# Small matrix products of the delta-rule heads issued by turns of four column steps, in one block per turn

## The chip, the cores and the metric

One core of a Trainium2 chip runs the whole program in a single launch. The metric is the device time of one execution in microseconds. The engines are named as in the profile: PE multiplies matrices (PEld loads its stationary operand), DVE is VectorE, ACT is ScalarE, POOL is GpSimd, SP issues most of the DMAs. Every engine works through its own queue in order, and waits where an operand or a buffer isn't ready.

## The reference

One block of a streaming encoder, in float32, for 512 frames of width 1024. What bears on the change is the first mixer, a gated delta rule with 8 heads of width 128 (condensed):

```python
h = rmsnorm(x, norm1_w)
q, k, v, z, b, a, glu, gates = split(h @ w_in)
q, k, v = silu(causal_conv4(concat(q, k, v)))            # 4 taps, per channel
q, k = l2norm(q), l2norm(k)
# per head: S_t = a_t S_{t-1} (I - b_t k_t k_t^T) + b_t k_t v_t^T,  o_t = q_t S_t
#   by chunks: triangular systems T u = b v inside a chunk, S carried from chunk to chunk
out_a = (rmsnorm(o) * silu(z)) @ w_o
c = ga * sigmoid(gb); c = silu(layernorm(causal_conv31(c)))
out_b = c @ w_pw2 + b_pw2
x = x + (sigmoid(gate_a) * out_a + sigmoid(gate_b) * out_b) @ w_out
x = rmsnorm(x + swiglu(rmsnorm(x)), norm_f_w)
```

## The kernel before

**Large products.** Every product with a weight matrix is split: each float32 operand becomes a high and a low part, and three products (high-high, high-low, low-high) are summed in PSUM. `split3` (L114 to L121) issues the three matmuls; for one column of weights (128 output channels, all 512 frames) there are eight such threes, one for each 128 of the input width. A *column step* is one of these threes. `unit` (L101) loads a column's weights, and splits them on ACT (L111, the high part) and DVE (L112, the low part); three such buffers rotate. The PSUM tiles `mm` of the columns rotate over three buffers too.

**The queue of columns.** The first stage of the program walks a queue of generators one column step at a time (`step`, and the counter `count`). For each head it holds the columns k, q, v and z (`head`; 32 steps), and then 12 or 8 steps of other columns (`take(OTHERS[h])`: the GLU columns of the convolution branch, then the gates). After the last head the other columns are run to the end. In all there are 481 counts. When a column ends its result is taken from PSUM: for k, q and v by `conv4` (L421 on ACT, three times L424 on DVE, a Silu at L427 on ACT), for z by a Silu (L793), for a GLU column at L657 and L662, for a gate by a sigmoid. The 31-tap convolution (`conv31`, L673, 30 DVE instructions a channel block) is traced far behind and fills DVE.

**Small products.** Between these large products stand the small ones of the heads, in plain float32, 128 columns wide or less. A product of four chunks is four calls, each of them two matmuls in the profile. For a head there are

- an *opening*, `front` (L437 transposes k, L470 is k k^T; ACT takes the squares, scales and stores U; a DRAM round trip on SP spreads U; POOL solves 16x16 systems at L506 and L508 into `y`), and `front2` (L437 transposes v, L519 is k q^T, L437 transposes q), which use the two PSUM buffers `g`;
- *merges* in `chain`, from 16x16 to 128x128 inverses: L545, L551, L568, L575, L587, L592, each with copies on ACT and DVE between, in the single PSUM buffer `b` (its results are collected in `Y`);
- the *recurrence* in `chain` over the four chunks n: L605 and L606 (from the second chunk on; DVE makes R at L608), L611 (ACT scales it to w at L613), L616 and L617 (DVE makes the next state S at L621 or L623 and the output o at L626 or L630, ACT an intermediate at L629), in the single PSUM buffer `st`;
- the end, `scaled` (four ACT instructions, L645) and `finish` (L437 transposes o into `b`, DVE L651 multiplies by z).

**What sets the order.** The text gives each instruction a place, and a planner puts each engine's queue together from that place and from when it takes operands to be ready; a small product that isn't ready is passed by large ones. `behind()` adds edges: what is traced inside it is issued, on its engine, after the last marked instruction (the large matmuls on PE; the splits L111 and L112; L424, the Silus and the sigmoids). `tc.issue_after(i)` adds one such edge of issue order, without a wait for `i` to finish. Generators yield the number of column steps until they are to be called again: a recurrence step yields 3, the merges between 1 and 4, and chain `h` starts at count `START + 32 h` and the other columns so far (START is 88). `front` runs at once when q is traced and two steps of v are done, `front2` five counts after z, with its three products together. `close()` is called between columns and runs `scaled` and `finish` some 32 counts after a chain's end.

Of the kernel before, what the change touches and what calls it, by code (L numbers as in the profile page):

```python
# [6 lines left out]
F32 = mybir.dt.float32  # L7
# [7 lines left out]
P = 128  # L15
# [8 lines left out]
PAD3 = 368  # L24
START = 88
ROUND = 40
WARM = 9
# [5 lines left out]
def block_kernel(ctx, tc, a):  # L33
# [65 lines left out]
    last = [None]  # L99

    def unit(ap, pool=None):  # L101

        aps = ap if isinstance(ap, tuple) else (ap,)
        n = T * len(aps) if isinstance(ap, tuple) else 1024
        raw, hi, lo = ((pool or wp).tile([P, n if pool else 1024], t, name=x)[:, 0:n]
                       for t, x in ((F32, "raw"), (F32R, "whi"), (F32R, "wlo")))
        for i, p in enumerate(aps):
            loads.append(nc.sync.dma_start(raw[:, i * T:(i + 1) * T] if len(aps) > 1 else raw, p))
        if start_feed[0]:
            fill()  # L110
        marked(S.activation(hi, raw, AF.Copy), "unit")  # L111
        marked(V.tensor_tensor(out=lo, in0=raw, in1=hi.bitcast(F32), op=ALU.subtract), "unit")  # L112
        return hi, lo

    def split3(ps, wt, xh, xl, first, last, mv=False):

        wh, wl = wt
        terms = ((wh, xh), (wh, xl), (wl, xh))
        for i, (w, m) in enumerate(terms):
            l, r = (m, w) if mv else (w, m)  # L120
            marked(PE.matmul(ps, l, r, start=first and i == 0, stop=last and i == 2))  # L121

# [269 lines left out]
    for t in (X, Y, Q1, Q2, Xd, Yd, Yl, Ye):  # L392
        G.memset(t, 0.0)
# [40 lines left out]
    def tok(src, pool, tag):  # L434
        ps = pool.tile([P, 4, P], F32, name=tag)
        for n in range(NT):
            PE.transpose(ps[:, n, :], src[:, n, :], ident)  # L437
        return ps
# [12 lines left out]
    def front(h, kT, DT):  # L451
# [17 lines left out]
        for n in range(NT):  # L469
            PE.matmul(ps[:, n, :], kT[:, n, :], kT[:, n, :], start=True, stop=True)  # L470
        Un = gp.tile([P, NT, P], F32, name="Un", bufs=3)
# [38 lines left out]

    def front2(kT, qT, vT, DT, ss):
        nk, sq = ss[:, 5], junk[:, 0:P]
        ps = tok(vT, psg, "g")
        Vp = gp.tile([P, NT, P], F32, name="Vp", bufs=3)
        for n in range(NT):
            S.activation(Vp[:, n, :], ps[:, n, :], AF.Copy, scale=nk[:, n:n + 1])
        ps = psg.tile([P, 4, P], F32, name="g")
        for n in range(NT):
            PE.matmul(ps[:, n, :], kT[:, n, :], qT[:, n, :], start=True, stop=True)  # L519
# [5 lines left out]
        return Vp, at  # L525

    def chain(h, kT, qT, ss, kd, b2, Un, Ud, Vp, at, yq, zs):
        sq = junk[:, 0:P]

# [12 lines left out]
        yield 2  # L542
        ps = psb.tile([P, 4, P], F32, name="b")
        for n in range(NT):
            PE.matmul(ps[:, n, 0:16], Ud[:, n, :], xc[:, n, 0:16], start=True, stop=True)  # L545
        Q0 = gp.tile([P, NT, 16], F32, name="Q0")
        S.activation(Q0, ps[:, :, 0:16], AF.Copy)
        yield 2
        ps = psb.tile([P, 4, P], F32, name="b")
        for n in range(NT):  # L550
            PE.matmul(ps[:, n, 0:16], Ye[:, n, :], Q0[:, n, :], start=True, stop=True)  # L551
        V.tensor_tensor(out=xc[:, :, 0:16], in0=xc[:, :, 0:16], in1=ps[:, :, 0:16], op=ALU.add)
        V.transpose(out=flat(y), in_=flat(xc))
        yield 1
        for i in range(2):
# [3 lines left out]
        for b in range(4):  # L559
            b32 = slice(32 * b, 32 * b + 32)  # L560
            S.copy(out=Y[b32, :, b32], in_=y[b32])
            if b < 2:
                S.copy(out=X[b32, :, b32], in_=xc[b32])


        ps = psb.tile([P, 4, P], F32, name="b")
        for n in range(NT):
            PE.matmul(ps[0:64, n, 0:64], Uc[:, n, :], Xd[:, n, :], start=True, stop=True)  # L568
        for i in range(2):
            s32 = slice(32 * i, 32 * i + 32)  # L570
            S.activation(Q1[s32, :, s32], ps[s32, :, s32], AF.Copy)
        yield 3
        ps = psb.tile([P, 4, P], F32, name="b")
        for n in range(NT):
            PE.matmul(ps[0:64, n, 0:32], Q1[:, n, :], Yd[:, n, :], start=True, stop=True)  # L575
        yield 1
        for i in range(2):
# [4 lines left out]
        S.copy(out=Yl[0:64], in_=Y[64:128, :, 64:128])  # L582
        yield 4

        ps = psb.tile([P, 4, P], F32, name="b")
        for n in range(NT):
            PE.matmul(ps[0:64, n, 0:64], Un[:, n, 64:128], X[:, n, :], start=True, stop=True)  # L587
        S.activation(Q2[0:64], ps[0:64, :, 0:64], AF.Copy)
        yield 3
        ps = psb.tile([P, 4, P], F32, name="b")  # L590
        for n in range(NT):
            PE.matmul(ps[0:64, n, 0:64], Q2[:, n, :], Yl[:, n, :], start=True, stop=True)  # L592
        V.tensor_copy(out=Y[0:64, :, 64:128], in_=ps[0:64, :, 0:64])
        yield 2

# [3 lines left out]
        for n in range(NT):  # L599
# [4 lines left out]
            else:  # L604
                PE.matmul(ps[:, 0, :], kT[:, n, :], Sp, start=True, stop=True)  # L605
                PE.matmul(ps[:, 2, :], qT[:, n, :], Sp, start=True, stop=True)  # L606
# [3 lines left out]
                yield 3  # L610
            PE.matmul(ps[:, 1, :], Y[:, n, :], R, start=True, stop=True)  # L611
            w = gp.tile([P, P], F32, name="w", bufs=2)
            S.activation(w, ps[:, 1, :], AF.Copy, scale=b2[:, n:n + 1])  # L613
            yield 3
            if n < NT - 1:
                PE.matmul(ps[:, 0, :], kd[:, n, :], w, start=True, stop=True)  # L616
            PE.matmul(ps[:, 3, :], at[:, n, :], w, start=True, stop=True)  # L617
            if n < NT - 1:
# [13 lines left out]
            if n < NT - 1:  # L632
                Sp = Sn
                yield 3

# [3 lines left out]
        tc.keep_in_program_order(G.tensor_tensor(out=ss[:, 4], in0=ss[:, 3], in1=half4, op=ALU.pow))  # L639
        ended.append([count[0], False, (h, o, ss, zs)])  # L640

# [89 lines left out]

    def close():

        if ended and count[0] - ended[0][0] > ROUND - 8:
            if ended[0][1]:
                finish(*ended.pop(0)[2])
            else:
                scaled(*ended[0][2])
                ended[0][1] = True

    def gates(a, b):
        for i in range(a, b):
            close()
            yield from gate(i)
# [29 lines left out]
    def head(h, done):  # L774

        pk, pq = (yield from proj2()) if h == 0 else (None, None)
        k_ = yield from conv4(8 + h, "kT", pk)
        close()
        q_ = yield from conv4(h, "qT", pq)
        close()  # L780
        v = conv4(16 + h, "vT")
# [14 lines left out]
        def second():  # L796
            Vp, at = front2(k_, q_, v_, DT, ss)
            done.append((h, k_, q_, ss, kd, b2, Un, Ud, Vp, at, y, z_))
            yield 0

        chains.append([count[0] + 5, second()])
        yield
# [12 lines left out]

    done, ended, dts, convs, count, chains = [], [], [], [], [0], [[0, decays()]]
    rest = others()
    for h in range(H):
        queue.append(head(h, done))
        queue.append(take(OTHERS[h]))  # L820
    queue.append(rest)
    nh = 0
    while step() or chains:
        start_feed[0] = count[0] >= 335
        if nh < H and count[0] >= START + 32 * nh + sum(OTHERS[:nh]):
            chains.append([0, chain(*done[nh])])
            nh += 1
        for c in list(chains):
            if c[0] <= count[0] or not queue:
                with behind():  # L830
                    n = next(c[1], None)
                if n is None:
                    chains.remove(c)
                else:
                    c[0] = count[0] + n
    background()
    for _, sc, e in ended:
        if not sc:
            scaled(*e)
        finish(*e)  # L840
    ph1.close()

# [527 lines left out]
```

## Time and profile before

| | us |
|---|---|
| median of 3 runs | 951.96 |
| lowest and highest | 951.70, 953.46 |
| the profiled execution's own time | 951.63 |
| its span, first to last instruction | 949.9 |
| PE busy in the span | 937.8 |
| stretch from the first opening to the last finish (53 to 464 us of the span) | 411.0 |

All times inside the profile are counted from the span's start. A row of grouped instructions gives line, engine, operation, output and inputs by the program's names, shape and count, then busy time, mean nanoseconds of one, and idle time before them with what ended it. A row of the timeline gives the start, the time until the group's end, and in brackets the idle time before it. A row of the chain gives start, duration and what ran. A row of stretches gives its borders, its length, each engine's busy time with its count of instructions, the granted clock and the DMA load. PE's ends are modelled, so a pitch (from one start to the next) says more than a duration.

### The profile page before, as it was taken

The numbers are of one execution on the slowest core, as the hardware profiler recorded it, in microseconds if no ns is written. First come the engines' busy times: TensorE is split into PE (matmuls) and PEld (weight loads), VectorE is DVE, ScalarE is ACT, GpSimd is POOL, SyncE is SP. The second block draws the span as 40 slices with busy tenths as digits, with TensorE's granted clock in tenths as the row PEclk, the third lists the DMA queues.
The fourth block names the chain that finished last, engine by engine and source line by source line (L and its number), as shares of the span: only waits on it lengthen the run. The fifth ranks groups of instructions, "written<-read, shape, count | busy, mean of one in ns | idle before, by whom it ended". The sixth has DMA issues, their size and how long they took to land.

```text
span 949.9 us, 14775 instructions
## 1 busy us (share of the span) xinstructions
PE 937.8 (99%) x5144; PEld 792.7 (83%) x5144; DVE 734.9 (77%) x1141; ACT 538.2 (57%) x1117; POOL 346.3 (36%) x548
## 2 busy tenths in 40 slices
PE   9999999999999999999999999999999999999996
PEld 6778888878888888888878888988889999988885
DVE  5899898888878898899688643675636877888896
ACT  7697785867877764643547222333334554556545
POOL 1136524344353347544154350254441111143042
PEclk9999999999999999999999999999999999999999
DMA  9234322322231346979899983599898565578654
GB/s 330 101 126 121 102 88 81 102 89 91 75 94 55 126 135 155 321 215 273 267 302 293 278 255 123 181 295 290 271 249 226 181 187 183 178 227 259 212 184 149
DMA packets 78187, 177.39 MB, mean 187 GB/s; under 512 B 10080, under 2 KB 19472, under 8 KB 77088
## 3 DMA queue, kind: packets, MB, share of 16 engines
q1 hardware_dynamic: 66528, 144.89, 46.0%
q0 software_dynamic: 10288, 28.90, 13.4%
q10 hardware_dynamic: 1296, 2.67, 0.7%
q8 instruction: 40, 0.66, 0.3%
q14 instruction: 35, 0.29, 0.1%
HBM read 156.22 MB, written 45.37 MB: 212 GB/s over the span
## 4 chain that ended last, share of the span: by engine, by line
PE 86%; ACT 3%; DVE 3%; issue 2%; POOL 1%; DMA 0%; POOLq 0%; DVEq 0%; ACTq 0%; SPq 0%
PE mm L121 56%; PE w L121 20%; PE g L437 1%; DVE wlo L112 1%; PE st L611 1%; PE st L617 1%; PE b L551 1%; PE b L545 1%; PE g L470 1%; PE st L616 1%; PE st L605 1%; PE st L606 1%; PE b L587 1%; PE b L592 1%; PE b L575 1%
## 5 line engine op out<-in xcount | busy, mean ns | idle before, releaser
L111 ACT ACTIVATE whi<-raw 128x1024 fp32r<-128x1024 f32 (+1 forms) x191 | 196.6, 1030 | 249.8 <-PE mm L121 160.3
L112 DVE TENSOR_TENSOR wlo<-raw,whi 128x1024 fp32r<-128x1024 f32 (+1 forms) x191 | 241.3, 1264 | 91.8 <-ACT whi L111 90.8
L121 PE MATMUL mm<-hh,whi 128*128 128x512 f32 (+1 forms) x688 | 269.8, 393 | 0.6 <-ACT hh L336 0.3
L121 PE MATMUL mm<-hh,wlo 128*128 128x512 f32 (+1 forms) x688 | 263.3, 383 | 0.0
L121 PE MATMUL mm<-hl,whi 128*128 128x512 f32 (+1 forms) x688 | 263.1, 382 | 0.0
L673 DVE SCALAR_TENSOR_TENSOR cps<-c,c31w,cps 128x512 f32<-128x512 f32 x240 | 180.2, 751 | 6.6 <-ACT cps L671 2.3
L121 PEld LDWEIGHTS mm<-hh,wlo 128*128 128x128 f32 x688 | 129.6, 188 | 23.6
L121 PEld LDWEIGHTS mm<-hh,whi 128*128 128x128 f32 x688 | 129.7, 189 | 22.7 <-issue 0.8
L121 PEld LDWEIGHTS mm<-hl,whi 128*128 128x128 f32 x688 | 129.9, 189 | 20.7
L1003 POOL TENSOR_TENSOR fm<-fm 128x256 f32<-128x256 f32 x33 | 29.9, 907 | 115.5 <-DVE s L1003 93.6
L424 DVE SCALAR_TENSOR_TENSOR acc<-mm,c4w,acc 128x511 f32<-128x511 f32 (+2 forms) x72 | 52.9, 739 | 2.8 <-ACT acc L421 2.6
L506 POOL TENSOR_TENSOR ytm<-U,y 128x60 f32<-128x60 f32 (+14 forms) x120 | 36.4, 303 | 50.6 <-DMA U<-sc 41.9
L121 PE MATMUL mm<-yh,whi 128*128 128x512 f32 x128 | 50.6, 396 | 0.0
L121 PE MATMUL mm<-yh,wlo 128*128 128x512 f32 x128 | 49.8, 389 | 0.0
L121 PE MATMUL mm<-yl,whi 128*128 128x512 f32 x128 | 49.8, 389 | 0.0
L121 PE MATMUL w<-hh,wlo 128*128 128x256 f32 x168 | 47.7, 284 | 0.3 <-DVE wlo L112 0.3
L121 PE MATMUL w<-hh,whi 128*128 128x256 f32 x168 | 47.6, 284 | 0.0
L121 PE MATMUL w<-hl,whi 128*128 128x256 f32 x168 | 47.5, 283 | 0.0
L196 POOL DMA_DIRECT2D s<-in_wgu_dram x24 | 23.4, 990 | 63.2 <-DMA s<-in_wgu_dram 63.2
L121 PE MATMUL w<-wlo,fh 128*128 128x512 f32 (+1 forms) x115 | 44.3, 385 | 0.1
L121 PE MATMUL w<-whi,fl 128*128 128x512 f32 (+1 forms) x115 | 44.2, 385 | 0.0
L121 PE MATMUL w<-whi,fh 128*128 128x512 f32 (+1 forms) x115 | 44.2, 385 | 0.0
(333 smaller groups left out, 1915.2 us busy)
## 6 DMA issues: line engine op xcount, KB each, us to landing
raw<-in_win_dram SPq DMA_DIRECT2D x61, 512.0 KB, 3.5
raw<-in_wgu_dram SPq DMA_DIRECT2D x32, 512.0 KB, 3.8
s<-in_wgu_dram SPq DMA_DIRECT2D x48, 256.0 KB, 5.6
raw<-s SPq DMA_DIRECT2D x48, 256.0 KB, 3.6
raw<-wsum SPq DMA_DIRECT2D x44, 256.0 KB, 3.6
raw<-in_wdn_dram SPq DMA_DIRECT2D x33, 256.0 KB, 3.2
s<-in_wgu_dram POOLq DMA_DIRECT2D x24, 256.0 KB, 7.4
s<-s POOLq DMA_DIRECT2D x24, 256.0 KB, 6.9
```

The lines of the kernel that those rows point to most:

```text
L111: marked(S.activation(hi, raw, AF.Copy), "unit")
L112: marked(V.tensor_tensor(out=lo, in0=raw, in1=hi.bitcast(F32), op=ALU.subtract), "unit")
L121: marked(PE.matmul(ps, l, r, start=first and i == 0, stop=last and i == 2))
L196: fed.append(nc.gpsimd.dma_start(*begun.pop(0), accum_op=ALU.add, max_dma_last_dim=2048))
L424: marked(V.scalar_tensor_tensor(out=acc[:, s:], in0=ps[:, :T - s], scalar=c4w[:, j, k:k + 1], in1=acc[:, s:], op0=ALU.mult, op1=ALU.add))
L437: PE.transpose(ps[:, n, :], src[:, n, :], ident)
L470: PE.matmul(ps[:, n, :], kT[:, n, :], kT[:, n, :], start=True, stop=True)
L506: G.tensor_tensor(out=tm[:, :, 0:w], in0=U[:, k, :, k + 1:], in1=y[:, :, k:k + 1].broadcast_to([P, NT, w]), op=ALU.mult)
L545: PE.matmul(ps[:, n, 0:16], Ud[:, n, :], xc[:, n, 0:16], start=True, stop=True)
L551: PE.matmul(ps[:, n, 0:16], Ye[:, n, :], Q0[:, n, :], start=True, stop=True)
L673: V.scalar_tensor_tensor(out=acc, in0=c[:, k:k + T], scalar=c31w[:, i, k:k + 1], in1=acc, op0=ALU.mult, op1=ALU.add)
L1003: return eng.tensor_tensor(out=out, in0=in0, in1=in1, op=op)
```

## The change

- *Turns.* Every fourth column step is a turn: 11 fixed offsets a head, also in a head with only 8 other steps (there the last three turns are three steps apart). Small products are issued only at turns, by `take_turn`: each running chain makes one step (recurrence or merge; the number that a generator yields no longer matters), then one waiting piece of an opening, then `scaled` or `finish` of an ended chain.
- *Chains.* A chain has 18 steps, and starts 11 turns after the one before it, the first at count 75 (`FIRST - 4`). So the last seven steps of a recurrence stand in the same turns as the seven merging steps of the next head. `Y` exists twice for that. `Yd` becomes a part of `Yl`. L551's copies now stand before the turn's end, L568 in the next turn; L575 and its copies are in one step.
- *Openings.* `front` waits for the next turn; `front2` is cut into two pieces (v's transposes and L519; q's transposes), one turn apart.
- *Ends.* `scaled` follows eight turns after the chain's end, `finish` at a later turn in which no chain is merging.
- *The hold.* `small_` remembers the last small product, and the first large product traced after it gets an edge of issue order behind it.

The core of the diff:

```diff
-START = 88
-ROUND = 40
+FIRST = 79
...
+    hold = [None]
+
+    def small_(b):
+        hold[0] = b
+        return b
...
-            marked(PE.matmul(ps, l, r, start=first and i == 0, stop=last and i == 2))
+            with tc.issue_after(hold[0].ins) if hold[0] else nullcontext():
+                marked(PE.matmul(ps, l, r, start=first and i == 0, stop=last and i == 2))
+            hold[0] = None
...
-    Y = gp.tile([P, NT, P], F32, name="Y")
+    Ys = [gp.tile([P, NT, P], F32, name="Y%d" % i) for i in range(2)]
...
-    Yd = gp.tile([P, NT, 32], F32, name="Yd")
     Yl = gp.tile([P, NT, 64], F32, name="Yl")
+    Yd = Yl[:, :, 0:32]
...
-            PE.transpose(ps[:, n, :], src[:, n, :], ident)
+            small_(PE.transpose(ps[:, n, :], src[:, n, :], ident))
...
         at = gp.tile([P, NT, P], F32, name="at", bufs=3)
         V.tensor_tensor(out=at, in0=ps, in1=DT, op=ALU.mult)
+        out += [Vp, at]
+        yield 1
         ps = tok(qT, psg, "g")
...
-                yield 3
+                yield 1
...
-        with behind(), tc.issue_after(last[0].ins) if h else nullcontext():
-            ss, kd, b2, Un, Ud, y = front(h, k_, DT)
+        made = []
+
+        def opening():
+            with tc.issue_after(last[0].ins) if h else nullcontext():
+                made.append(front(h, k_, DT))
+            yield
+
+        pending.append(opening())
...
-        chains.append([count[0] + 5, second()])
+        pending.append(second())
...
+        n = 32 + OTHERS[h]
+        turns += [at_ + o for o in ((3, 7, 11, 15, 19, 23, 27, 31, 35, 39, 43) if n == 44 else
+                                    (3, 7, 11, 15, 19, 23, 27, 31, 34, 37, 40))]
+        at_ += n
+    turns += range(at_ + 3, at_ + 300, 4)
...
+    def take_turn():
+        merging = False
+        turn[0] += 1
+        for c in list(chains):
+            merging |= c[0] < 7
+            with behind():
+                if next(c[1], None) is None:
+                    chains.remove(c)
+            c[0] += 1
+        if pending:
+            with behind():
+                if next(pending[0], None) is None:
+                    pending.pop(0)
+        if ended and turn[0] - ended[0][0] > 7:
+            if not ended[0][1]:
+                scaled(*ended[0][2])
+                ended[0][1] = True
+            elif not merging:
+                finish(*ended.pop(0)[2])
...
+        if count[0] in turns or not queue:
+            if nh < H and (turn[0] - first if first is not None else 0 if count[0] >= FIRST - 4 else -1) >= 11 * nh:
+                first = turn[0] if first is None else first
+                chains.append([0, chain(*done[nh])])
+                nh += 1
+            take_turn()
```

More of the change, by code (lines that the diff above doesn't have):

```diff
@@ L796, in second @@
         def second():
[L797 to L801 removed]
+            ss, kd, b2, Un, Ud, y = made[0]
+            both = []
+            yield from front2(k_, q_, v_, DT, ss, both)
+            done.append((h, k_, q_, ss, kd, b2, Un, Ud, *both, y, z_))
+            yield
+        pending.append(second())
         yield
@@ L813, in take @@
             yield
-    done, ended, dts, convs, count, chains = [], [], [], [], [0], [[0, decays()]]
+    done, ended, dts, convs, count, pending, turn = [], [], [], [], [0], [], [0]
     rest = others()
+    turns, at_ = [], 0
     for h in range(H):
@@ L820, in block_kernel @@
         queue.append(take(OTHERS[h]))
-    queue.append(rest)
-    nh = 0
-    while step() or chains:
-        start_feed[0] = count[0] >= 335
[L825 to L835, printed above, removed]
+        n = 32 + OTHERS[h]
[3 more added lines that the diff above has]
+    turns += range(at_ + 3, at_ + 300, 4)
+    turns = set(turns)
+    queue.append(rest)
+    chains, nh, opened, dec = [], 0, [0], decays()
+    def take_turn():
[17 more added lines that the diff above has]
+                finish(*ended.pop(0)[2])
+    first = None
+    while step() or chains or pending:
+        start_feed[0] = count[0] >= 335
+        if dec and count[0] in (1, 3):
+            with behind():
+                dec = None if next(dec, None) is None else dec
+        if count[0] in turns or not queue:
[4 more added lines that the diff above has]
+            take_turn()
     background()
@@ L840, in block_kernel @@
         finish(*e)
+    hold[0] = None
     ph1.close()
```

64 lines of the change are left out of this document (26 added, 38 removed).

## The prediction

> **What bounds the kernel now.** I read the page first, then the stretch in which heads are computed, then PE's own order in it.
>
> ```profile
> span 949.9 us, 14775 instructions
> ...
> PE 937.8 (99%) x5144; PEld 792.7 (83%) x5144; DVE 734.9 (77%) x1141; ACT 538.2 (57%) x1117; POOL 346.3 (36%) x548
> ```
>
> ```profile
> 53.00:464.00 411.00, 408.67 (x2250) 335.74 (x2249) 353.55 (x636) 278.51 (x737) 189.21 (x383) 1.00 0.45 137
> ```
>
> PE is the bound: 99% of the span. The second row is the stretch that the change touches: 411.0 us long, PE busy 408.7 (its engines in order: PE, PEld, DVE, ACT, POOL), the granted clock 1.00. A busy PE can still start its matmuls late, so pitches decide. The chain of waits gives the undisturbed pitch of large products:
>
> ```profile
> 436.57 27.25 PE mm L121 x120
> ```
>
> 27.25 us / 120 = 0.227 us. The lines of the stretch hold 446 products in each of three terms:
>
> ```profile
> L121 PE MATMUL mm<-hh,wlo 128*128 128x512 f32 x446 | 176.7, 397 | 0.0
> ```
>
> 3 x 446 x 0.227 = 303.7 us, so 411.0 - 303.7 = 107.3 us go to the small products and to waiting. What one interruption costs is read from the timeline, PE alone, around two of them:
>
> ```profile
> 410.49 0.40 PE L121 MATMUL mm<-hh,wlo 128*128 128x512 f32 x1
> 410.73 0.38 PE L611 MATMUL st<-Vp,Y 128*128 128x128 f32 x2
> 410.87 0.48 PE L121 MATMUL mm<-hh,whi 128*128 128x512 f32 x1
> 411.18 0.39 PE L121 MATMUL mm<-hl,whi 128*128 128x512 f32 x1
> ...
> 412.80 0.39 PE L121 MATMUL mm<-hh,wlo 128*128 128x512 f32 x1
> 413.02 0.38 PE L616 MATMUL st<-w,kd 128*128 128x128 f32 x2
> 413.24 0.39 PE L617 MATMUL st<-w,at 128*128 128x128 f32 x2
> 413.38 0.48 PE L121 MATMUL mm<-hh,whi 128*128 128x512 f32 x1
> 413.70 0.40 PE L121 MATMUL mm<-hl,whi 128*128 128x512 f32 x1
> ```
>
> From the large product before to the second large product after, less two pitches: 411.18 - 410.49 - 0.454 = 0.236 us for two small matmuls, 413.70 - 412.80 - 0.454 = 0.446 for four. So a small matmul costs 0.105 us and **an interruption by itself only 0.026**.
>
> **The change, part by part.** *Fewer interruptions.* Walking PE's timeline I count 145 stretches of small matmuls between large ones, from the first row below to the last:
>
> ```profile
> 53.69 0.49 PE L437 MATMUL g<-cst,kT 128*128 128x128 f32 x3
> ...
> 463.66 0.60 PE L437 MATMUL b<-cst,o 128*128 128x128 f32 x4
> ```
>
> After: four turns with openings alone (heads 0 and 1), 94 consecutive turns of which each has a step of a recurrence or a merge (chain 0's second step to chain 7's last: 7 x 11 + 17), and the last head's finish: 99. The number of small matmuls does not change. 46 fewer x 0.026 = **-1.2 us**.
>
> One rule of the Trainium skill would make even this nothing: by "TensorE: Matmul & The Clock Gate", Part 2, the engine pulls weight loads ahead of matmuls in flight, so a switch of shapes should be free; then the term is 0 instead of -1.2. The two differences above say 0.026, not 0.
>
> *Waits that go.* Priced the same way, 24 of the 145 stretches cost over 0.04 us more than their own matmuls, 5.0 us together. The two kinds:
>
> ```profile
> 69.06 0.39 PE L121 MATMUL mm<-hh,wlo 128*128 128x512 f32 x1
> 69.87 0.66 PE L437 MATMUL g<-cst,qT 128*128 128x128 f32 x4 [0.43 <-ACT Vp L516]
> 70.28 0.48 PE L121 MATMUL mm<-hh,whi 128*128 128x512 f32 x1
> 70.60 0.40 PE L121 MATMUL mm<-hl,whi 128*128 128x512 f32 x1
> ...
> 272.43 0.39 PE L121 MATMUL mm<-hl,whi 128*128 128x512 f32 x1
> 273.19 0.49 PE L605 MATMUL st<-S,kT 128*128 128x128 f32 x2 [0.37 <-DVE o L630]
> 273.51 0.39 PE L606 MATMUL st<-S,qT 128*128 128x128 f32 x2
> 273.65 0.47 PE L121 MATMUL mm<-hh,wlo 128*128 128x512 f32 x1
> 273.97 0.39 PE L121 MATMUL mm<-hh,whi 128*128 128x512 f32 x1
> ```
>
> Both stretches hold four matmuls (0.446) and took 70.60 - 69.06 - 0.454 = 1.086 and the same at 273: 0.64 too much each. In the first, q's transposes wait for a PSUM buffer that v's evictions hold; six such add up to 1.8 us. After, they stand one turn later, 12 large products x 0.227 = 2.7 us. In the second, the recurrence, one step in three (9 products, 2.0 us), waits for its single PSUM tile; with the merges of a column step or two it makes 1.9 us. A turn gives 2.7 us plus the turn's own small products. I let both kinds go: **-3.7 us**; bounds 0 and all 5.0. Of the remaining 1.3 I move nothing.
>
> *The hold.* Now a small product finds its place by readiness, and large ones pass it:
>
> ```profile
> 276.43 0.80 PE b L545 x8
> 277.23 6.91 PE mm L121 x30
> ...
> 285.69 0.80 PE b L551 x8
> ```
> ```profile
> 284.17 0.21 ACT L547 ACTIVATE Q<-b 128x64 f32<-128x64 f32 x1
> ```
>
> L551 was due 6 products (1.4 us) after L545; its operand Q was copied only at 284.17, and 30 products ran in one piece meanwhile. After, the first product of the next column step stands behind the turn's last small one, and with it the rest of its column, which accumulates in order. What can still pass is another column, if its weights are split and PSUM is free. It does so today:
>
> ```profile
> 43.09 0.97 PE L121 MATMUL mm<-hh,whi 128*128 128x512 f32 x3 [0.34 <-ACT hh L336]
> ```
>
> Three first terms in a row are three columns. So in the steady state I put the hold at 0, covered by the following columns.
>
> At head 0 that cover is missing. Its opening moves to the turn after v's sixth column step, 66 products into the projections instead of 54; but k is not there yet:
>
> ```profile
> 50.97 1.28 ACT L427 ACT_TABLE_LOAD   x1
> 52.27 0.63 ACT L427 ACTIVATE kT<-acc 128x512 f32<-128x512 f32 x1
> ```
> ```profile
> 51.59 1.21 DVE L112 TENSOR_TENSOR wlo<-raw,whi 128x1024 fp32r<-128x1024 f32 x1
> ```
>
> k ends at 52.90. Counting large products on the timeline from the first one of these projections, 82 had run when the opening came at 53.69: 28 more than the 54 behind which the text has it slid past. Held behind 66, PE comes to it 16 products earlier; k lets it start about two products before 53.69, so PE lacks work for 14. The next column, z, has its low half only from 51.59 + 1.21 = 52.80; two terms of z fit before that. (14 - 2) x 0.227 = **+2.7 us**; bounds 0 (z's split comes earlier) and 3.2 (no cover).
>
> *At nothing.* The second Y replaces Yd: one more zeroing on POOL, off PE's path. Chain 0 starts 13 column steps earlier; y(0) was done long before:
>
> ```profile
> 87.29 0.21 POOL L508 TENSOR_TENSOR y<-y,ytm 128x4 f32<-128x4 f32 x1
> ```
> ```profile
> 95.97 0.34 ACT L533 ACTIVATE yb<-y,cst 128x64 f32<-128x64 f32 x1
> ```
>
> 8.5 us of slack; 13 steps are 39 products, 8.9 us, so the slack is used up and y(0) comes just in time. If it comes late, the first merge slips by what is missing, an estimated 0.4 us (8.9 - 8.5), once. No DMA is added: U's loads move with the openings by up to four column steps (2.7 us) and SP's queue order is the same; DVE and ACT execute the same instructions.
>
> Sum against the profiled execution, 951.63 us (span 949.9 and 1.7 around it): -1.2 - 3.7 + 2.7 = -2.2, so 949.4; its time is 0.3 under the median 951.96, which gives **949.7 us**.
>
> **The rivals.** *A, the holds cost (slower).* Place: the turn behind L611 of the second chunk, which comes 6 products after v's projection ends. Its eviction w is queued on ScalarE behind v's Silu:
>
> ```profile
> 254.07 0.68 ACT L421 ACTIVATE acc<-mm,c4w 128x512 f32<-128x512 f32 x1
> ...
> 262.26 0.66 ACT L427 ACTIVATE vT<-acc 128x512 f32<-128x512 f32 x1
> ...
> 263.07 0.39 ACT L613 ACTIVATE w<-st,ss 128x128 f32<-128x128 f32 x1
> ```
>
> From the start of L421 to w's end 9.4 us; L616 is due 18 products and two small ones after v's end, 4.3 us, so it is 5 us late. Over heads 2 to 7 the Silu ends 4.5 to 8.8 us after L421 starts; with w the lateness sums to 15.3 us. Six products of the next column are unheld (1.36 us a head); if nothing else passes, 8.3 us stay: 949.7 + 8.3 = 958.0. For it: eviction latencies decide, not PE. Against: three columns interleave at 43.09. It decides from the point at which the columns behind the next one have no PSUM.
>
> *B, cleaner than I think.* Head 0's hold is covered and all 5.0 us of waits go: 951.96 - 1.2 - 5.0 = 945.8. Against: this wait at head 0 is ScalarE's lateness, which no turn mends.
>
> ```profile
> PE g L437 <- ACT vT L427: 0.6, 1, 0.6
> ```
>
> *C, it does not do what it says.* Small products stay where readiness puts them, other columns fill in between, the stretches stay near 145 and waits only change places; head 0's hold against half of the 5.0 us of waits: 951.96 + 2.7 - 2.5 = 952.2.
>
> *D, the clock.* A hold that idles PE long enough costs a slow restart. At the kernel's start:
>
> ```profile
> 1.00 3.49 PE L258 MATMUL g<-one 128*128 128x512 bf16 x9 [1.00 <-DVE epsc L73]
> ```
>
> Nine took 3.49 us instead of 9 x 0.227 = 2.04: 1.45 us for a cold start; with head 0's 2.7 us and no waits saved, 951.96 + 2.7 + 1.45 - 1.2 = 954.9. The rule ("TensorE: Matmul & The Clock Gate", Part 1) halves the clock after an idle window of about 3.4 us; no wait shown here is near that, and the 2.7 would be under it.
>
> **How the numbers follow.** Forecast 0.38, A 0.20, B 0.16, C 0.23, D 0.03. A measurement here tells about 0.2% (1.9 us) from no change: 950.1 and 953.9 are the bounds. Faster: B, 0.28 of the forecast's (its own range 947 to 951.5 crosses 950.1), 0.03 of C: 0.47. Slower: A without 0.02, D, 0.05 of C: 0.26. Same: the rest, 0.27. The range leaves out half of A and the edge of B: 945.5 to 957.
>
> **What would show it.** On PE's timeline: some 99 stretches, not 145; at head 0 a gap before L437 that ends with kT (right) or none (B); no wait of L437 for Vp and none of L605 for o (the -3.7). A shows as PE idle before L616 with w as releaser, near the end of v's projections. The forecast is wrong if PE's waits in 53 to 464 grow instead of shrinking, or if the time after 464 moves.

## The result: 1.1% slower

The changed kernel takes 962.75 us (median of 4 runs, 962.0 to 963.76), the one before 952.71 us beside it (951.7 to 953.59): ratio 1.0108, 95% interval 1.0096 to 1.012. Forecast were 949.7 us and a range up to 957. The profiled execution took 962.98 us.

The same two rows of the page as before, and the same stretch by windows (us, then PE, PEld, DVE, ACT, POOL busy, PE's granted clock):

```profile
span 961.2 us, 14776 instructions
...
PE 939.5 (98%) x5144; PEld 797.3 (83%) x5144; DVE 734.0 (76%) x1141; ACT 532.6 (55%) x1113; POOL 335.5 (35%) x548
```
```profile
53.00:464.00 411.00, 399.96 (x2207) 332.67 (x2206) 351.69 (x635) 269.25 (x726) 181.40 (x382) 1.00 0.41 130
```

PE executes the same 5144 instructions. In the 411 us between 53 and 464 it was busy 408.67 us before and is busy 399.96 now: 8.7 us more in which it does nothing, and 43 matmuls fewer done (2207 against 2250), at the same full clock. All other engines did a little less too: nobody is busier, somebody waits for somebody. PE's waits by line and releaser:

```profile
PE mm L127 <- DVE acc L431: 5.4, 4, 2.2
PE g L444 <- ACT vT L434: 1.3, 2, 0.7
PE mm L127 <- DVE ss L472: 1.2, 1, 1.2
...
PE mm L127 <- DVE ss L470: 0.8, 1, 0.8
PE mm L127 <- DVE sm L761: 0.6, 1, 0.6
PE st L618 <- DVE R L615: 0.6, 1, 0.6
PE st L623 <- ACT w L620: 0.5, 1, 0.5
PE b L583 <- ACT Q L579: 0.4, 1, 0.4
```

The large waits are not those of small products. They are first products of *new columns* (L127 writing mm) that wait for a PSUM buffer until VectorE's tap instructions (L431) have read a column out. The rows that name ss or sm belong to them: in each, the instruction named stands right behind a column's last tap in VectorE's queue. Together that is 8.0 us. The old kinds, L437 for Vp and L605 for o, are gone from these rows, as forecast, though a wait for o of 0.3 us now stands at L618. The same in the page's list of groups, first the kernel before, then the changed one:

```profile
L121 PE MATMUL mm<-hh,whi 128*128 128x512 f32 (+1 forms) x688 | 269.8, 393 | 0.6 <-ACT hh L336 0.3
...
L127 PE MATMUL mm<-hh,whi 128*128 128x512 f32 (+1 forms) x688 | 271.4, 395 | 8.3 <-DVE acc L431 5.4
```

One of these places, PE, VectorE and ScalarE by the timeline:

```profile
262.85 0.38 PE L618 MATMUL st<-R,Y 128*128 128x128 f32 x2
...
265.60 0.39 PE L127 MATMUL mm<-hh,wlo 128*128 128x512 f32 x1
268.16 0.47 PE L127 MATMUL mm<-hh,whi 128*128 128x512 f32 x1 [2.17 <-DVE acc L431]
...
269.15 0.39 PE L623 MATMUL st<-w,kd 128*128 128x128 f32 x2
```
```profile
265.18 0.72 DVE L431 SCALAR_TENSOR_TENSOR acc<-mm,c4w,acc 128x511 f32<-128x511 f32 x1
...
265.96 0.74 DVE L431 SCALAR_TENSOR_TENSOR acc<-mm,c4w,acc 128x510 f32<-128x510 f32 x1
...
267.28 0.74 DVE L431 SCALAR_TENSOR_TENSOR acc<-mm,c4w,acc 128x509 f32<-128x509 f32 x1
```
```profile
266.00 1.14 ACT L480 ACTIVATE Un<-g,ss 128x128 f32<-128x128 f32 x4 [1.21 <-DVE ss L472]
268.11 0.63 ACT L434 ACTIVATE vT<-acc 128x512 f32<-128x512 f32 x1 [0.97 <-DVE acc L431]
268.65 0.35 ACT L620 ACTIVATE w<-st,ss 128x128 f32<-128x128 f32 x1
```

This is the turn behind L618 of the second chunk, rival A's place. L618's result is in PSUM at 263.2, but w, its scaled copy, is made at 268.65, right behind v's Silu (268.11) in ScalarE's queue, and that Silu waits for the last tap of v on VectorE. L623 needs w. The rows don't name the column of a product; from the order of PE's queue I read what ran meanwhile: 12 products of one column (262.99 to 265.83), until its next product is one that is held behind L623; a second column stands in the same way, with 3 products done. The third PSUM buffer still holds v, which the last tap reads until 268.02. A new column starts at 268.16, does three products, and only then comes L623. So passing did take place, 12 products of it, and ended when three buffers were all taken.

For the whole stretch I walked PE's timeline from the first product with hh to the first with yh (1440 large products of 0.227 us, 326.9 us, in each kernel) and divided what is more than that: extra time around small products (their own time and their waits), and waits between two large ones. All in us; the kernels in the lower rows follow below:

| kernel | stretches of small products | extra around small ones | waits between large ones | whole stretch |
|---|---|---|---|---|
| before | 146 | 106.4 | 3.3 | 436.5 |
| changed | 111 | 107.9 | 12.0 | 446.8 |
| changed, no hold (e1_no_hold) | 110 | 103.4 | 2.7 | 432.9 |
| changed, v's Silu free (e2_silu_free) | 110 | 104.5 | 4.1 | 435.5 |
| both (e5_both) | 111 | 102.7 | 2.8 | 432.4 |
| no hold, one-piece opening (e11_one_piece) | 113 | 104.1 | 2.6 | 433.5 |
| before, opening in two pieces (e7_before_split) | 141 | 106.8 | 3.2 | 436.9 |
| changed, a turn later (e9_hold_shift) | 109 | 113.0 | 8.9 | 448.8 |
| that, q's and v's Silus free (e13_shift_qv_free) | 105 | 106.7 | 18.4 | 452.1 |
| that, v's taps free too (e15_shift_taps_free) | 113 | 108.1 | 5.5 | 440.5 |

From before to changed: +1.5 around small products, +8.7 in waits between large ones. After the stretch nothing moved: from its end to the span's end it is 949.9 - 469.6 = 480.3 us before and 961.2 - 480.9 = 480.3 us now. Another 1.0 us lies ahead of the stretch's first product. That start falls between 33.0 and 34.9 us in the kernels of the table, with the hold or without, so I don't count it as an effect of the change.

### The profile page after: what moved, and what is told of

Its sections match the earlier page's. It is cut to its first block, busy times and chain, and to the rows that moved or that the text cites. A ratio compares the mean times of both kernels' runs of the same rounds, so it can differ in the third digit from the quotient of the medians.

```text
span 961.2 us, 14776 instructions
## 1 busy us (share of the span) xinstructions
PE 939.5 (98%) x5144; PEld 797.3 (83%) x5144; DVE 734.0 (76%) x1141; ACT 532.6 (55%) x1113; POOL 335.5 (35%) x548
## 4 chain that ended last, share of the span: by engine, by line
PE 83%; DVE 6%; ACT 3%; issue 2%; DMA 0%; POOL 0%; POOLq 0%; ACTq 0%; DVEq 0%; SPq 0%
PE mm L127 54%; PE w L127 20%; DVE acc L431 2%; DVE cps L680 2%; DVE wlo L117 1%; PE g L444 1%; PE g L526 1%; PE st L624 1%; PE b L559 1%; PE b L553 1%; ACT whi L116 1%; PE st L618 1%; PE st L612 1%; PE st L623 1%; PE g L477 1%
## 5 line engine op out<-in xcount | busy, mean ns | idle before, releaser
L127 PE MATMUL mm<-hh,whi 128*128 128x512 f32 (+1 forms) x688 | 271.4, 395 | 8.3 <-DVE acc L431 5.4
L127 PE MATMUL mm<-hh,wlo 128*128 128x512 f32 (+1 forms) x688 | 261.3, 380 | 0.0
L127 PE MATMUL mm<-hl,whi 128*128 128x512 f32 (+1 forms) x688 | 260.8, 379 | 0.0
L127 PEld LDWEIGHTS mm<-hh,whi 128*128 128x128 f32 x688 | 129.6, 188 | 33.6 <-issue 6.4
L127 PEld LDWEIGHTS mm<-hh,wlo 128*128 128x128 f32 x688 | 129.4, 188 | 25.3
L127 PEld LDWEIGHTS mm<-hl,whi 128*128 128x128 f32 x688 | 129.9, 189 | 20.6
L431 DVE SCALAR_TENSOR_TENSOR acc<-mm,c4w,acc 128x511 f32<-128x511 f32 (+2 forms) x72 | 53.2, 742 | 6.6 <-ACT acc L428 6.4
L127 PE MATMUL mm<-yh,whi 128*128 128x512 f32 x128 | 50.6, 396 | 0.0
L513 POOL TENSOR_TENSOR ytm<-U,y 128x60 f32<-128x60 f32 (+14 forms) x120 | 31.9, 266 | 52.9 <-DMA U<-sc 44.1
L127 PE MATMUL mm<-yh,wlo 128*128 128x512 f32 x128 | 49.8, 389 | 0.0
L127 PE MATMUL mm<-yl,whi 128*128 128x512 f32 x128 | 49.8, 389 | 0.0
L127 PE MATMUL w<-hh,wlo 128*128 128x256 f32 x168 | 47.7, 284 | 0.3 <-DVE wlo L117 0.3
L127 PE MATMUL w<-hh,whi 128*128 128x256 f32 x168 | 47.6, 284 | 0.0
L127 PE MATMUL w<-hl,whi 128*128 128x256 f32 x168 | 47.5, 283 | 0.0
L127 PE MATMUL w<-wlo,fh 128*128 128x512 f32 (+1 forms) x115 | 44.3, 386 | 0.1
L127 PE MATMUL w<-whi,fh 128*128 128x512 f32 (+1 forms) x115 | 44.2, 385 | 0.0
L127 PE MATMUL w<-whi,fl 128*128 128x512 f32 (+1 forms) x115 | 44.2, 385 | 0.0
```

What stands on the lines that cost most here:

```text
L431: marked(V.scalar_tensor_tensor(out=acc[:, s:], in0=ps[:, :T - s], scalar=c4w[:, j, k:k + 1], in1=acc[:, s:], op0=ALU.mult, op1=ALU.add))
L513: G.tensor_tensor(out=tm[:, :, 0:w], in0=U[:, k, :, k + 1:], in1=y[:, :, k:k + 1].broadcast_to([P, NT, w]), op=ALU.mult)
```

## The experiments

Every kernel here computes the whole block. Line numbers move by one to four between them.

**The hold alone taken away (e1_no_hold).** The turns, the two `Y`s and the split opening stay.

```diff
     def small_(b):
-        hold[0] = b
         return b
```

> The changed kernel with its turns, but without the edge that holds the next large product behind a turn's last small one. Theory 1 (the hold costs: columns that pass a held column fill the three PSUM buffers, and PE then stands before a new column until DVE's L431 has drained one): the 8.8 us of waits between large products shrink to under 1.5 us and the time falls from 962.8 to 953 to 955 us. Theory 2 (the turns cost: evictions that are bunched on DVE and ACT delay the draining of the columns, hold or not): the waits on L431 stay at 5 us or more, 959 to 963 us.

Measured: 949.33 us (10 runs) against 952.51, ratio 0.9966 (0.9957 to 0.9976). That is below the 953 to 955 us that I expected, because I had counted only the waits between large products. The hold costs 962.75 - 949.33 = 13.4 us, and everything else in the change is a small gain of 3.2 us. By the table the hold puts 12.0 - 2.7 = 9.3 us into waits between large products and 107.9 - 103.4 = 4.5 us into those around small ones. Not one wait of a large column for L431 is left in its rows; what PE still waits for in this stretch is, but for 0.2 us, head 0's v (the wait for Vp is back, too):

```profile
PE g L443 <- ACT vT L433: 0.6, 1, 0.6
...
PE g L443 <- ACT Vp L522: 0.4, 1, 0.4
```

**The suspected lateness alone taken away (e2_silu_free).** The hold stays; v's Silu is no longer one of the marked instructions, so that w, which is traced inside `behind()`, may come ahead of it on ScalarE. (So may any other small work of ScalarE that is traced there; the edit isn't limited to w.)

```diff
-        marked(S.activation(o.rearrange("p n t -> p (n t)"), acc, AF.Silu))
+        s_ = S.activation(o.rearrange("p n t -> p (n t)"), acc, AF.Silu)
+        if name != "vT":
+            marked(s_)
```

> The changed kernel with its hold, but v's Silu (L434) no longer marked, so that the eviction w (L620) of the second chunk may be queued on ScalarE ahead of it. Theory 1 with this place (five of the large waits, 7.6 us, stand shortly before L623 of the second chunk in heads 3 to 7): most of these go, 955 to 958 us. If the place is another one (the DVE work behind k's and q's ends), or by theory 2: at most 1.5 us better, 961 to 963 us.

Measured: 951.31 us (10 runs) against 952.51, ratio 0.9988 (0.9978 to 0.9997), better than the 955 to 958 us that I expected. With the hold in place, taking this one mark off is worth 11.4 of the 13.4 us. ScalarE in the same head, by the timeline:

```profile
257.90 0.37 ACT L622 ACTIVATE w<-st,ss 128x128 f32<-128x128 f32 x1
...
262.19 0.65 ACT L434 ACTIVATE vT<-acc 128x512 f32<-128x512 f32 x1
```

This is the same chunk's w; it now runs 4.3 us ahead of the Silu (262.19 - 257.90). What the hold still costs is 951.31 - 948.55 = 2.8 us (against the kernel with both edits, next).

**Both, and the Silu in the kernel before (e5_both, e8_before_silu).** The same two edits together; and the second one alone in the old kernel.

> The changed kernel without the hold and with v's Silu unmarked. If both earlier results are two ends of one chain (w late behind the Silu, and a hold that turns lateness into a wait), the second adds little where large products may pass: 948 to 950 us. If the Silu's edge costs for another reason, the gains add up: below 947 us.

> The kernel before with v's Silu unmarked, nothing else. Without a hold large products pass a late w, so its lateness should cost nothing there: 951.5 to 953.5 us. If the place in ScalarE's queue matters without the hold too: 2 us or more better, below 950.7.

Measured: 948.55 us, ratio 0.996 (0.9945 to 0.9975); and 951.98 us, ratio 0.9991 (0.9981 to 1.0). Where small products aren't held, the Silu's place is worth 0.8 us or less, which these runs don't tell from none. The Silu was ahead of w before, too; nobody paid for it, since large products passed. With `e1_no_hold`'s interval overlapping, 948.55 us is the lowest median here, and a version that is 0.4% faster than the kernel before.

**All three Silus free, no hold (e10_free_all).** The marks of k's, q's and v's Silus are taken off `e1_no_hold`.

> The changed kernel without the hold and with none of the three Silus (k, q, v) put among the urgent small work of ScalarE. If what is left of the lateness of w and o on ScalarE counts, 947 to 949 us; if the Silus themselves are then late for the normalisation and the transposes, 949 to 953 us.

Measured: 949.32 us, ratio 0.9961 (0.9949 to 0.9974): no different from one Silu or none.

**The hold put into the old kernel (e3_before_hold).** `small_` and the edge in `split3`, without turns.

> The kernel before with the hold alone: all its small products as before, spaced by one to four column steps, and the next large product behind the last small one. Theory 1: before, large products passed late small ones by up to 31; held, columns interleave and PSUM runs out, 958 to 970 us, with waits of large products on L431's DVE drains. Theory 2: the hold alone costs nothing, 952 to 954 us.

Measured: 1065.71 us, ratio 1.1185 (1.1168 to 1.1202), 113 us more, far over the 958 to 970 us that I expected. The largest waits, and the granted clock:

```profile
PE st L624 <- ACT w L621: 19.1, 7, 4.4
PE mm L128 <- DVE acc L432: 11.2, 4, 4.9
```
```profile
core 0: 1064.4 us, clock 0.955
```

Places written as "so many counts behind" are due times for products that may slide; taken literally, many merges and recurrence steps come due before their operands. Not all of the 113 us are waits: at a clock of 0.955 on average, 82 large products of the stretch follow each other after 0.43 us instead of 0.227, which is 16 us. With turns, whose steps lie 2.7 us and more apart in most places, a hold costs 13.4 us; without them 113.

**A strict hold (e4_strict).** The edge isn't cleared after the first large product: every later one stands behind the last small one too, and no column can pass.

```diff
-            hold[0] = None
```

> The changed kernel with a strict hold: every later large product, of whatever column, stands behind the last small one traced before it. No column can pass, so PSUM can't run out. Theory 1: the waits move from large products (on L431) to small ones (on w, R, o and the copies): the lateness of w alone was put at 15.3 us, 965 to 980 us. Theory 2: waits on L431 stay before large products, 961 to 964 us.

Measured: 986.65 us, ratio 1.0354 (1.0338 to 1.0369), over the 965 to 980 us of theory 1.

```profile
PE st L622 <- ACT w L619: 10.4, 6, 2.5
PE g L443 <- ACT vT L433: 7.4, 1, 7.4
PE st L617 <- DVE o L636: 3.2, 1, 3.2
PE g L443 <- ACT kT L433: 2.6, 1, 2.6
```

With passing forbidden, both stalls that I had worked out come out bare: w six times with 10.4 us (put at 15.3), and kT at head 0 with 2.6 us (forecast: 2.7). The 7.4 us for head 0's vT I had not priced. Letting other columns pass was worth 986.65 - 962.75 = 23.9 us in the changed kernel: large, but not the whole. Some 4.4 of them are large products at half clock (22 of them 0.43 us apart), of which the changed kernel has none.

**A fourth column buffer (e6c_acc_sbuf, e6_psum4).** The convolution's accumulator moves from PSUM to SBUF (the control), and then every fourth column takes the bank that this frees.

```diff
-        acc = psc.tile([P, T], F32, name="cps")
+        acc = gp.tile([P, T], F32, name="cps")
 ...
+        cols[0] += 1
-        ps = psm.tile([P, T], F32, name="mm")
+        ps = psc.tile([P, T], F32, name="mx") if cols[0] % 4 == 0 else psm.tile([P, T], F32, name="mm")
```

> Control for the next kernel: the changed kernel with its hold, the accumulator of the 31-tap convolution in SBUF instead of PSUM, Un with two buffers instead of three. Nothing that the theories speak of changes: 961 to 964 us.

> The control, with the PSUM bank that came free used as a fourth one for columns (every fourth column takes it). If the held columns exhaust three PSUM buffers, a fourth lets columns pass further: the waits of large products fall from 8.8 to under 3 us, 954 to 958 us. If it is the draining itself that is late (each column waits for its own drain whatever the number of buffers): as the control.

Measured: 990.19 us for the control and 985.59 us with the fourth buffer. The control itself lost 27 us, so the pair says little of sizes. What it does show: the 14.2 us of waits of columns for a buffer in the control's rows

```profile
PE mm L127 <- DVE ss L472: 7.8, 4, 2.3
PE mm L127 <- DVE acc L431: 6.4, 3, 2.8
```

are gone with the fourth one, and in their place stand waits for weight splits and for small products' operands:

```profile
PE st L621 <- DVE o L640: 4.8, 2, 4.6
PE mm L127 <- DVE wlo L117: 4.7, 5, 1.8
PE mm L127 <- ACT whi L116: 3.1, 1, 3.1
```

So the buffers were indeed what ended the passing; with one more, the lateness is paid at the next thing that runs out. The time fell by 4.6 us, against 14.2 us of waits that went. How much of the 4.6 is the buffer's I can't say: large products at half clock fell from 5.0 to 0.6 us between the two profiles as well.

**The chains one turn later (e9_hold_shift, e14_shift_no_hold).** w's turn is then no longer the one behind v's Silu.

```diff
-FIRST = 79
+FIRST = 83
```

> The changed kernel with its hold, and the chains' first turn put one turn (four column steps) later, so that the turn of w and the last merge no longer comes right behind the second chunk's v Silu. The theory that the loss is the place (w queued behind that Silu, the held product ahead of it, passing columns filling the three PSUM buffers) expects the waits of the large products before L623 of the second chunk to go and 953 to 957 us; what is left of the hold is then other lateness. The rival, that the hold costs wherever the turns stand, expects 961 to 964 us with such waits at other lines.

> The changed kernel with the chains one turn later and without the hold. The theory that the turn's place costs only where products are held expects 948.5 to 951 us. The rival, that the later chains cost by themselves (a later finish of each head), expects 953 us or more.

Measured: 965.42 us with the hold (ratio 1.0135, 1.0119 to 1.015), and 949.78 us without it (0.9973, 0.9963 to 0.9983). My expectation of 953 to 957 us was wrong, and the rival's 961 to 964 lies nearer: the place wasn't one bad slot that a shift avoids. The later place by itself costs nothing that these runs tell from none. In the held kernel's trace, other operands stand at the same kind of place. VectorE around the v of head 4 (the place shown above was around the v of head 5):

```profile
220.28 0.74 DVE L431 SCALAR_TENSOR_TENSOR acc<-mm,c4w,acc 128x511 f32<-128x511 f32 x1
...
222.07 0.74 DVE L431 SCALAR_TENSOR_TENSOR acc<-mm,c4w,acc 128x510 f32<-128x510 f32 x1
...
223.54 0.72 DVE L431 SCALAR_TENSOR_TENSOR acc<-mm,c4w,acc 128x509 f32<-128x509 f32 x1
...
224.32 0.35 DVE L615 SCALAR_TENSOR_TENSOR R<-st,sm,Vp 128x128 f32<-128x128 f32 x1
```

R, the operand of L618, now waits behind v's three taps on VectorE; and on ScalarE w of the first chunk follows q's Silu:

```profile
218.14 0.62 ACT L434 ACTIVATE qT<-acc 128x512 f32<-128x512 f32 x1
218.66 0.35 ACT L620 ACTIVATE w<-st,ss 128x128 f32<-128x128 f32 x1
```

New theory: any eviction of the projections ahead of a held product's operand costs, on either engine.

**The two taken apart (e13_shift_qv_free, e15_shift_taps_free).** The shifted kernel with q's and v's Silus free; then v's taps (L431) not marked as well, which lets R, and other small work of VectorE, go ahead of them or between them. The edit for the taps:

```diff
-            marked(V.scalar_tensor_tensor(out=acc[:, s:], ...
+            s_ = V.scalar_tensor_tensor(out=acc[:, s:], ...
+            if name != "vT":
+                marked(s_)
```

> The changed kernel with its hold, the chains one turn later, and the Silus of q and v not put among the urgent work of ScalarE. In the trace of the shifted kernel two things wait: small products of w behind q's Silu (the small products' excess grew by 6.6 us against the kernel before), and passing columns that run out of PSUM while R stands on VectorE behind v's tap instructions (8.9 us of waits between large products, 3.3 before). The theory that any eviction of the projections ahead of a held product's operand costs, on either engine, expects the first to go and the second to stay: 956 to 961 us. The rival that only Silus count expects 949 to 953 us; the rival that the hold costs by itself, whatever the operands, expects 964 to 967 us.

> The shifted kernel with the hold and the Silus of q and v free (967.3 us), and v's three tap instructions on VectorE also not put among the urgent work, so that R of the second chunk comes ahead of one or all of them in VectorE's queue. The theory that the 18.4 us of waits between large products come from R standing behind v's taps expects most of them to go: 951 to 957 us. The rival, that the held turn costs by itself or that PSUM is short because v's eviction is late (now later still), expects 962 us or more.

Measured: 967.32 us (1.0159, 1.0145 to 1.0173), outside the 956 to 961 us that I expected and next to the 964 to 967 of a hold that costs by itself; and 956.19 us (1.0038, 1.0025 to 1.0052), which that rival put at 962 or more. In the first, ScalarE's half went as expected (around small products 113.0 to 106.7, -6.3 us), but VectorE's half grew from 8.9 to 18.4 us (1.6 of it large products at half clock, told at the end). Head 4 again, PE and VectorE:

```profile
223.88 0.39 PE L127 MATMUL mm<-hh,wlo 128*128 128x512 f32 x1
227.08 0.47 PE L127 MATMUL mm<-hh,whi 128*128 128x512 f32 x1 [2.81 <-DVE acc L431]
...
227.62 0.38 PE L620 MATMUL st<-R,Y 128*128 128x128 f32 x2
```
```profile
226.19 0.74 DVE L431 SCALAR_TENSOR_TENSOR acc<-mm,c4w,acc 128x509 f32<-128x509 f32 x1
226.85 0.34 DVE L617 SCALAR_TENSOR_TENSOR R<-st,sm,Vp 128x128 f32<-128x128 f32 x1
```

v's last tap moved from 223.54 to 226.19, while the recurrence step whose result R is made from came at nearly the same time (220.42 there, 220.93 here). (Why the taps came later, with convolution work and a split between them, I did not test.) With the taps' marks off, the waits between large products fall from 18.4 to 5.5 us, the time by 11.1 us. In that trace, in the same head, the product that reads R runs before v's last tap:

```profile
218.90 0.39 PE L622 MATMUL st<-R,Y 128*128 128x128 f32 x2
```
```profile
219.98 0.74 DVE L431 SCALAR_TENSOR_TENSOR acc<-mm,c4w,acc 128x509 f32<-128x509 f32 x1
```

So small work of VectorE behind v's taps is the second form of the stall, and R is the one of it that the rows show; that it is R alone, this edit can't tell. What is left above the unheld 949.78 is 6.4 us, which I did not take apart.

**The opening in one or two pieces (e7_before_split, e11_one_piece).** The one saving of the forecast that can be tried alone: the old kernel with q's transposes four counts later; and the unheld new one with `front2` in one piece again.

```diff
         V.tensor_tensor(out=at, in0=ps, in1=DT, op=ALU.mult)
+        out += [Vp, at]
+        yield 4
         ps = tok(qT, psg, "g")
```

> The kernel before with one edit: the next head's opening cut in two, the q transposes a few column steps behind the k and v ones. The prediction's step of 1.8 us expects 950.0 to 951.5 us against 952.6 and no waits of the transposes for Vp. The rival expects no change, because the stretch that it adds and its interruptions take back what the waits gave.

> The changed kernel without the hold and with the next head's opening in one piece again, as before the change. The prediction's step that puts 1.8 us on the q transposes which no longer wait for Vp expects 950.5 to 951.5 us against 949.33 without the hold, and waits of L437 or its like for Vp in the trace. The rival, that those waits were short because other work covered them, expects 949 to 950 us.

Measured: 952.58 us against 953.0 (0.9996, 0.9988 to 1.0005), no change; and 950.3 us (0.9973, 0.9962 to 0.9984) where the two pieces gave 0.9966 (0.9957 to 0.9976), not told apart. I had put 1.8 us on q's transposes. The rows of before name 0.7 us of such waits, in two places. Head 0's 0.4 us is still there in both of these kernels; in the first:

```profile
PE g L437 <- ACT Vp L516: 0.4, 1, 0.4
```

## Why the prediction was wrong

**The step that failed** is "in the steady state I put the hold at 0, covered by the following columns". It costs 13.4 us in all (e1_no_hold), of which 11.4 go when small work of ScalarE, w above all, may pass v's Silu (e2_silu_free). My evidence was three first terms in a row at 43.09. By their count they are the last steps of k and q, which head 0 runs side by side (products 43 and 44 of their 48), and the first of v: one column *starting* while the third PSUM buffer was free. At the place that matters one buffer is still being read by v's taps, and the two others belong to columns whose next products are themselves held behind the small product that waits. I had the two facts in hand, three `mm` buffers and an eviction that lasts until v's last tap, and did not lay them over the place that I priced in rival A.

**Rival A** had the place, the releaser (w behind v's Silu) and even the point from which it decides ("the columns behind the next one have no PSUM"). It was given 0.20 and 8.3 us. Measured, head 0 included: 9.3 us of waits between large products, and 4.5 more around small ones that it did not price (L618 for R 0.6 us, L583 for Q 0.4 us in the rows of waits): once the products are held, each late operand of any kind shows. My sign for it was wrong in form: "PE idle before L616 with w as releaser" is 0.5 us; the rest appears as columns that wait for a buffer, named after VectorE.

**Fewer interruptions, -1.2.** 35 or 36 fewer stretches, not 46: at 0.026 us that is -0.9. It can't be seen apart in a time. The stretches beyond my 99, I did not trace.

**Waits that go, -3.7.** By the same pricing as in the prediction, the stalls of 5.0 us are about 3.1 us without the hold: -1.9, give or take 0.3 by how a small matmul is priced. With -0.9 that is -2.8, and the extra around small products fell by 106.4 - 103.4 = 3.0, the time by 3.2 us. So both terms together are 3 us, where I had 4.9; the part on q's transposes (1.8) is one that the two runs on it alone did not find.

**Head 0, +2.7.** There is no gap ahead of the opening, 75 large products into the projections; others than the held column covered it. But near it stand two waits, 0.6 and 1.0 us:

```profile
51.94 0.47 PE L127 MATMUL mm<-hh,whi 128*128 128x512 f32 x1 [0.63 <-DVE sm L761]
...
54.10 0.60 PE L444 MATMUL g<-cst,kT 128*128 128x128 f32 x4
...
62.72 0.47 PE L127 MATMUL mm<-hh,whi 128*128 128x512 f32 x1 [0.98 <-DVE acc L431]
```

The same two are there in e2_silu_free, e9_hold_shift, e13_shift_qv_free and e15_shift_taps_free, and in no kernel without the hold. The size of the stall is confirmed by the strict hold, 2.6 us; the cover that I gave it was too small, as the one of the other heads was too large.

That 949.33 us without the hold lies near 949.7 is no merit: -3.2 stands where I had -4.9 + 2.7.

**The rivals B, C, D.** B is refuted for the kernel as changed; the best variant, 948.55, remains 2.7 us above its time. C is wrong in its first half: the stretches did fall to 111. D did not happen in the changed kernel: the granted clock stays at 1.00 in the stretch. In five other held kernels some large products did run at half clock: 16 us more for it in e3_before_hold, 0.6 to 5.0 us in e4_strict, e6c_acc_sbuf, e6_psum4 and e13_shift_qv_free.

## What to carry to other kernels

When work that could slide is pinned in an in-order queue, the price is the lateness of its operands minus what may still pass; count the buffers that the passing work needs at that very moment, the one still being evicted and the ones behind the pin included. Then look at what stands ahead of the operand on its own engine: here the pin costs 2.8 us instead of 13.4 once the operand is let past one Silu, while moving the pin by one turn only gave it another eviction to stand behind. Without a pin the same order of small products, grouped by turns, was worth 3 us.

## What the runs showed of the chip

*A short idle can halve PE's clock, or not.* In e13_shift_qv_free PE idled 2.10 us ahead of 269.27; about 1 us after it the windows view has a granted clock of half (it stands behind the five busy times):

```profile
267.00:269.30 2.30, 0.20 (x2) 0.06 (x1) 2.30 (x9) 1.54 (x7) 1.01 (x1) 1.00 0.49 153
...
270.30:272.00 1.70, 1.70 (x5) 1.32 (x4) 1.60 (x3) 0.78 (x4) 1.10 (x1) 0.50 0.00 0
```

From 270.33 to 272.04 large products come every 0.43 us instead of 0.227. The idle of 2.81 us ahead of 227.08 in the same run, and that of 2.17 us in the changed kernel, were followed by products at the full 0.23 us. Over all traces of this case, each of the 16 idles of 3.16 us and more between 5 and 600 us was followed within 4 us by large products at half clock; of those between 1.8 and 3.12 us, some were and some weren't. The Trainium skill ("TensorE: Matmul & The Clock Gate", Part 1) has the clock halved after an idle window of about 3.4 us, in windows that run freely. The half rate agrees with the 0.50 here. The length doesn't: 2.1 us was enough and 2.8 wasn't, both under the page's; what decides between them, no run here shows. In the prediction's rival D I took it for safe that no wait was near that length.

*With an accumulator in SBUF two engines are slower.* With the 31-tap convolution's accumulator in SBUF instead of PSUM (e6c_acc_sbuf) each tap takes 828 ns (750 in the changed kernel), and POOL's products at L513 take 448 ns on average, where the changed kernel has 266 and the other kernels with the accumulator in PSUM up to 331:

```profile
L680 DVE SCALAR_TENSOR_TENSOR cps<-c,c31w,cps 128x512 f32<-128x512 f32 x240 | 198.7, 828 | 4.7 <-ACT cps L678 0.3
```
```profile
L513 POOL TENSOR_TENSOR ytm<-U,y 128x60 f32<-128x60 f32 (+14 forms) x120 | 53.7, 448 | 51.0 <-DMA U<-sc 42.2
```

Both engines slow down together where these taps of VectorE work on SBUF alone, and again in e6_psum4 (818 and 486 ns); why, no run here shows. The kernel took 27 us longer, with 5 us of large products at half clock among them and with one buffer fewer for Un, which was not tried alone.
